# Latent norms of the MLA layer: the last chunk's squares go to the ones-products directly, one strip step later

## The chip, the cores and the metric

The kernel runs on one core of one Trainium2 chip. The metric is device time in microseconds (us) of a whole execution, as the median of several runs. One execution is recorded by the hardware profiler; its rows give start times from the start of the span.

## What is computed

The program is a two-layer encoder trunk on a sequence of 1024 tokens of width 1024, in f32. Layer 0 is differential attention and layer 1 is multi-head latent attention. The change is in layer 1, in the norms of its two latents:

```
proj = h @ w_in
q_a, c_kv, k_pe, z = split(proj, [384, 384 + 256, 384 + 256 + 64])
q  = (_rmsnorm(q_a,  q_a_norm_g)  @ w_q_b)     # 384 features: 3 chunks of 128
kv = (_rmsnorm(c_kv, kv_a_norm_g) @ w_kv_b)    # 256 features: 2 chunks of 128
_rmsnorm(x, g): x * rsqrt(mean(x * x, axis=-1) + 1e-6) * g
```

For each token the squares of all features of a latent are summed. The features lie on partitions here, so the sum over a chunk's 128 features needs a product with ones on TensorE, and the chunks' sums have to be added.

## The kernel before, in words

Every f32 product is made of three fp32r products of 128 x 512 (`mm3`, L186 to L188): high by high, low by high, high by low. `gen_half` makes one output chunk of 128 features by one half of the tokens (512) in eight strip steps, each one `mm3` over 128 input features, so 24 products, and then hands the PSUM bank `acc` to a consumer. The weight strips come by DMA (`wraw`), are cast to their high part by ScalarE (`wh`, L231), and the low part is a subtraction on GpSimd (`wl`, L232).

`lora` makes a latent: strips 1 to 3 for the first (three chunks), 4 and 5 for the second (two chunks), each in two halves. Its consumer `put` copies `acc` to `craw` and squares it, both on ScalarE. For chunk 0 the squares go into the tile `csum`; for every later chunk they go into a tile `csq`, and VectorE adds `csq` to `csum` (L1402). `norm(half)` then makes four small products (128x1, L1407): each takes 128 tokens' columns of `csum` as the stationary operand and a column of ones as the moving one, and puts the sums into the PSUM tile `cps`. VectorE makes `c_w` from it (L1409), GpSimd raises it to the power of minus a half (`rq_y`), two DMAs spread the row over the partitions (`bc_d`, `bc_s`), VectorE scales `craw` (L1416), ScalarE casts its high part (`c_h`, L1424), VectorE subtracts (L1425) and two DMAs write both to `cS`.

There are four norms: two latents by two halves. A norm isn't issued where its chunk ends but within the next half: `half_and_norm` calls what is waiting in `norms` after the strip step with number `NORM_AT` (4, so after five of eight steps). The order of the instructions on each engine is fixed when the program is built; each engine works its list in order and waits at an instruction whose inputs are not there.

Beside the latents VectorE works on `combos`: sums and differences `t1` to `t4` of the input for the gate branch that follows, each with a cast on ScalarE and a subtraction on VectorE (L1341 to L1350). Behind the latents come the first strips of the gate branch (`silu_gate`: `zth` on ScalarE, `gz` on VectorE, L783), then `z_pair`, whose products (`zacc`) take weights that VectorE combines first (`zs`, `zraw`, L1493 to L1496). `load_wk` splits the weights of the values in between (`wvh` on VectorE, `wvl` on GpSimd, L1554 and L1555).

Of the kernel before, what the change touches and what calls it, by code (L numbers as in the profile page):

```python
# [21 lines left out]
P = 128  # L22
# [22 lines left out]
V_LATE = 6  # L45
MODS = (2, 1, 1, 1, 0, 0, 0, 0)
V1_AT = (3, 2)
NORM_AT = 4
PRE0 = (0, 0, 0, 0, 2, 1, 2, 2, 2, 2, 1)
PRE_N = 6  # L50
PRE1 = (0, 0, 0, 0, 0, 0, 0, 1, 1, 1, 1)
# [28 lines left out]
def f32v(ap):  # L80
    return ap.bitcast(F32)
# [3 lines left out]
def trunk(ctx: ExitStack, tc: tile.TileContext, A, out):  # L85
    nc = tc.nc
    SP, PE, V, S, G = nc.sync, nc.tensor, nc.vector, nc.scalar, nc.gpsimd
# [31 lines left out]
    def bank(tag, name, shape=None):  # L119
        nonlocal turn  # L120
        if tag == "acc":
            turn += 1
            if (turn - 1) % (2 + NB.get("accx", 0)) < 2:
                return psa.tile([P, HF], F32, name=name, tag="acc", bufs=2)
            tag = "accx"
        return ps.tile(shape or [P, HF], F32, name=name, tag=tag, bufs=NB[tag])
# [19 lines left out]
    ones = const.tile([P, P], F32, name="ones")  # L146
# [23 lines left out]
    def rsqrt(w, n):  # L170

        y = sm.tile([P, n], F32, name="rq_y")
        G.tensor_tensor(out=y, in0=w, in1=mhalf[:, :n], op=ALU.pow)
        return y
# [231 lines left out]
    def bcast_rows(sp, y, tag, bufs):  # L406

        d_ = dr.tile([HF], F32, name="bc_d", tag="bcd", bufs=4)
        SP.dma_start(d_.rearrange("(p t) -> p t", p=P), y)
        b = sp.tile([P, HF], F32, name="bc_s", tag=tag, bufs=bufs)  # L410
        SP.dma_start(b, d_[None, :].to_broadcast([P, HF]))
        return b, b.rearrange("p (q t) -> p t q", t=4)

    def t3(ap_):
        return ap_.rearrange("p (t q) -> p t q", t=4)
# [838 lines left out]
    w4, h1f, lm = [], {}, {}  # L1254

    def strip1(i, wpool=None):
        return load_strip([A["w_s1"][i, f] for f in range(2)], [4, 4], wpool)
# [40 lines left out]
    def rpt(name, dt=F32):  # L1298
        return wp.tile([P, HF], dt, name=name, tag="rp", bufs=6)
# [76 lines left out]
    def run_norms():  # L1376
        for f in norms[:]:
            norms.remove(f)
            f()

    def half_and_norm(w, half, consume):

        for k, _ in enumerate(gen_half(w, h1, half, consume)):
            side.tick()
            if k == NORM_AT:
                run_norms()

    def lora(idx, dst, gvec, width, ws=None, first=None):
        n = len(idx)
        craw = [[None, None] for _ in range(n)]  # L1390
        sums = [None, None]
        def put(i, half, acc):
            t = rpt("craw") if dst and i == 0 else lr.tile([P, HF], F32, name="craw", tag="craw", bufs=7)
            S.copy(t, acc)
            craw[i][half] = t
            if i == 0:
                sums[half] = lr.tile([P, HF], F32, name="csum", tag="csum", bufs=2)
                lm["S"] = S.activation(sums[half], acc, AF.Square).ins
            else:
                s2 = rpt("csq")  # L1400
                lm["S"] = S.activation(s2, acc, AF.Square).ins
                lm["V"] = V.tensor_add(sums[half], sums[half], s2).ins  # L1402

        def norm(half):
            pt = bank("tr", "cps", [P, 4, P])
            for j in range(4):
                PE.matmul(pt[:, 0, j : j + 1], sums[half][:, j * P : (j + 1) * P], ones[:, 0:1], start=True, stop=True)  # L1407
            wv = sm.tile([P, 4], F32, name="c_w")
            V.tensor_scalar(wv, pt[:, 0, 0:4], 1.0 / width, EPS, op0=ALU.mult, op1=ALU.add)  # L1409
            y = rsqrt(wv, 4)  # L1410
            _, rb = bcast_rows(wp, y, "rp", 6)

            def rest():
                for i in range(n):
                    t = craw[i][half]
                    tc.keep_in_program_order(V.scalar_tensor_tensor(  # L1416
                        out=t3(t), in0=t3(t), scalar=gvec[:, i : i + 1], in1=rb, op0=ALU.mult, op1=ALU.mult))
                norms.append(split)

            def split():  # L1420
                for i in range(n):
                    t = craw[i][half]
                    hi = p4.tile([P, HF], F32R, name="c_h", tag="zraw", bufs=6)
                    S.copy(hi, t)  # L1424
                    V.tensor_sub(t.bitcast(F32R), t, f32v(hi))  # L1425
                    SP.dma_start(cS[dst + i, half, 0], f32v(hi))
                    SP.dma_start(cS[dst + i, half, 1], t)

            norms.append(lambda: norms.append(rest))

        for i, si in enumerate(idx):
            w = strip1(si) if i or ws is None else ws
            for half in range(2):
                if (i, half) == (0, 0) and first:
                    first(lambda acc: put(0, 0, acc))
                else:
                    half_and_norm(w, half, lambda acc: put(i, half, acc))
                if i == n - 1:
                    norms.append(lambda half=half: norm(half))
# [18 lines left out]

    p4 = None
    lora((1, 2, 3), 0, qag, QL, w4[1], first_halves)  # L1460
    zraw = []

    def z_fetch(p, parts):
        for m, f in parts:
            raw = p4.tile([P, HF], F32, name="zraw", tag="zraw", bufs=6)
            SP.dma_start(raw, A["w_s1"][6 + 2 * p + m, f])
            zraw.append(raw)

    lora((4, 5), 3, kvg, KVL)
    for h in range(2):  # L1470
        w = strip1(6 + h)
# [417 lines left out]
    class Pre7:  # L1889
        n = 0  # L1890
# [295 lines left out]
```

## Time and profile before

| what | value |
|---|---|
| median of three runs | 1426.74 us (1424.81 to 1427.36) |
| the profiled execution's own time | 1425.08 us |
| its span | 1423.3 us |
| granted TensorE clock over the span | 0.996 |
| PE busy, VectorE busy, ScalarE busy, GpSimd busy | 1387.4, 935.2, 730.0, 658.4 us |
| first and last start of the four norms' small products | 828.1 and 865.3 us |

In the rows PE is TensorE's matmul, PEld its weight load, DVE is VectorE, ACT ScalarE, POOL GpSimd, SP the engine that issues the DMAs. A row of the timeline has start, duration, engine, source line, operation, output and inputs, shape, and in square brackets how long the engine sat idle before it and who ended that. Spacing between two starts on PE is the better measure of what a product costs, since the shown ends are modelled and overlap the next product.

### The profile page before, as it was taken

Reading aid. Unit: us, or ns where it says so; the run is one execution under the profiler, and the core shown is the slowest. Engines: PE = TensorE matmul, PEld = TensorE weight load, DVE = VectorE, ACT = ScalarE, POOL = GpSimd, SP = SyncE. Lnnn points to the kernel's source line nnn. Section 1 sums busy time; section 2 is a strip of 40 time slices with the busy share of each in tenths; the row PEclk is TensorE's granted clock in tenths of the full one; section 3 lists DMA queues with packets and bytes.
Section 4 is the critical chain, followed back from the end, with each engine's and each line's share of the span. In section 5 each row is a group of like instructions: output and inputs, shape, how many; then the busy total and the mean of one; then the engine's idle time right before and its main releaser. Section 6 shows DMA issues by size and latency. Waiting matters only on the chain. (4 is left out here: it accounts for less than half of the span.)

```text
span 1423.3 us, 20684 instructions
## 1 busy us (share of the span) xinstructions
PE 1387.4 (97%) x7366; PEld 1155.7 (81%) x7366; DVE 935.2 (66%) x1364; ACT 730.0 (51%) x1299; POOL 658.4 (46%) x520
## 2 busy tenths in 40 slices
PE   9999999999999999998999999999999999999997
PEld 6777788888888887886788777887888888888886
DVE  8665777777777777677435886545666655555685
ACT  5523465656565655566343543335454454545554
POOL 5425254646464646453561324532131165653683
PEclk9999999999999999999999999999999999999999
DMA  9786633333332323236572136398544355566363
GB/s 346 246 244 199 192 88 112 82 112 104 111 112 89 90 90 90 89 101 232 201 221 108 55 111 203 121 301 239 158 124 120 101 166 185 182 212 210 130 252 119
DMA packets 141722, 222.35 MB, mean 156 GB/s; under 512 B 19762, under 2 KB 56754, under 8 KB 141619
## 3 DMA queue, kind: packets, MB, share of 16 engines
q1 hardware_dynamic: 141618, 221.03, 49.2%
q8 instruction: 58, 0.95, 0.3%
q14 instruction: 46, 0.37, 0.1%
HBM read 141.07 MB, written 56.31 MB: 139 GB/s over the span
## 5 line engine op out<-in xcount | busy, mean ns | idle before, releaser
L386 ACT CAST pth<-tr 128x512 fp32r<-128x512 f32 x256 | 150.1, 586 | 288.0 <-PE tr L384 286.2
L401 DVE TENSOR_REDUCE nm<-s 128x1 f32<-128x1024 f32 x192 | 234.0, 1219 | 73.3 <-PE s L848 61.5
L387 DVE TENSOR_TENSOR ptl<-tr,pth 128x512 fp32r<-128x512 f32 x256 | 176.1, 688 | 140.4 <-ACT pth L386 139.8
L232 POOL TENSOR_TENSOR wl<-wraw,wh 128x512 fp32r<-128x512 f32 (+2 forms) x79 | 104.9, 1330 | 211.3 <-ACT wh L231 198.8
L403 ACT ACTIVATE e<-s,nm 128x1024 f32<-128x1024 f32 x128 | 143.6, 1122 | 28.8 <-DVE nm L401 26.6
L384 PE MATMUL tr<-ident,e 128*128 128x128 f32 x1024 | 155.7, 274 | 2.4 <-DVE ptl L387 2.1
L384 PEld LDWEIGHTS tr<-ident,e 128*128 128x128 f32 x1024 | 121.3, 140 | 44.3 <-DVE ptl L387 20.2
L186 PE MATMUL acc<-h0h,wh 128*128 128x512 f32 x360 | 149.8, 416 | 1.1 <-ACT wh L231 0.6
L186 PE MATMUL pv<-pth,vt 128*128 128x256 f32 x512 | 147.8, 289 | 0.0
L187 PE MATMUL pv<-ptl,vt 128*128 128x256 f32 x512 | 145.8, 285 | 0.0
L188 PE MATMUL pv<-pth,vt 128*128 128x256 f32 x512 | 144.6, 282 | 0.0
L188 PE MATMUL acc<-h0h,wl 128*128 128x512 f32 x360 | 143.2, 398 | 0.4 <-POOL wl L232 0.4
L187 PE MATMUL acc<-h0l,wh 128*128 128x512 f32 x360 | 141.9, 394 | 0.0
L187 PEld LDWEIGHTS pv<-ptl,vt 128*128 128x128 f32 x512 | 97.6, 191 | 3.0 <-DVE ptl L387 0.2
L186 PEld LDWEIGHTS pv<-pth,vt 128*128 128x128 f32 x512 | 97.5, 190 | 3.0 <-ACT pth L386 0.4
L188 PEld LDWEIGHTS pv<-pth,vt 128*128 128x128 f32 x512 | 97.5, 191 | 0.1
L328 POOL TENSOR_TENSOR rp_r<-rp_raw,cosT 128x512 f32<-128x512 f32 x38 | 50.0, 1315 | 89.7 <-ACT rp_raw L325 37.9
L333 POOL TENSOR_TENSOR rp_sw<-rp_sw,sinT 128x512 f32<-128x512 f32 x42 | 55.4, 1319 | 70.5 <-DMA rp_sw<-rp_raw 68.0
L848 PE MATMUL s<-ks,qa 128*128 128x512 f32 x256 | 82.3, 403 | 3.8 <-DVE e L856 2.2
L856 DVE SCALAR_TENSOR_TENSOR e<-s,z,e 128x1024 f32<-128x1024 f32 x64 | 82.1, 1283 | 2.0
L848 PE MATMUL s<-ks,qb 128*128 128x512 f32 x256 | 80.7, 396 | 0.0
L188 PEld LDWEIGHTS acc<-h0h,wl 128*128 128x128 f32 x360 | 67.6, 188 | 16.1 <-POOL wl L232 0.8
(505 smaller groups left out, 3406.7 us busy)
## 6 DMA issues: line engine op xcount, KB each, us to landing
ada<-in_ada_ss SPq DMA_DIRECT2D x32, 512.0 KB, 5.6
wraw<-in_w_s SPq DMA_DIRECT2D x64, 256.0 KB, 2.9
vS<-v_hl SPq DMA_DIRECT2D x32, 512.0 KB, 5.9
vt<-vS SPq DMA_DIRECT2D x32, 512.0 KB, 4.3
rp_sw<-rp_raw SPq DMA_DIRECT2D x168, 64.0 KB, 2.0
bc_s<-bc_d SPq DMA_DIRECT2D x34, 256.0 KB, 3.8
wor<-in_w_out SPq DMA_DIRECT2D x32, 256.0 KB, 4.3
wol<-tS SPq DMA_DIRECT2D x28, 256.0 KB, 4.9
```

The source lines that it names most:

```text
L186: PE.matmul(psum, ah, bh, start=first, stop=False, skip_group_check=skip)
L187: PE.matmul(psum, ah, bl, start=False, stop=False, skip_group_check=skip)
L188: mm3.last = PE.matmul(psum, al, bh, start=False, stop=last, skip_group_check=skip).ins
L232: sub = (V if pair_of else G).tensor_sub(l_[:, :n], raw[:, :n], f32v(h_[:, :n]))
L333: in_turn(G.tensor_mul(sw, sw, sinT[:, cs]))
L384: PE.transpose(tr[:, j, :], p[:, kt * P : (kt + 1) * P], ident)
L386: mk["S"] = S.copy(pth[kh][:, :, dst], tr).ins
L387: mk["V"] = V.tensor_sub(ptl[kh][:, :, dst], tr, f32v(pth[kh][:, :, dst])).ins
L401: mk["V"] = V.reduce_max(nm, s_ps, axis=AX.X, negate=True).ins
L403: mk["S"] = S.activation(e, s_ps, AF.Exp, bias=nm, scale=1.0, accum_out=zs).ins
L848: PE.matmul(s_ps[:, kc * HF : (kc + 1) * HF], src[:, c, ql], KS[h][kc][:, c, :], start=fst, stop=not fst)
L856: combined.append(V.scalar_tensor_tensor(out=e0, in0=e1, scalar=z1[:, 0:1], in1=e0, op0=ALU.mult, op1=ALU.add).ins)
```

## The change

In a latent's last chunk the squares are no longer added to `csum` on VectorE. They stay in their own tile, and `norm` makes eight small products in place of four: for each 128 tokens one with `csum` and one with the last chunk's `csq`, summed in PSUM. For the first latent that leaves one addition per half on VectorE, for the second latent none. `NORM_AT` goes from 4 to 5, so that a norm is issued after six of eight strip steps.

```
-NORM_AT = 4
+NORM_AT = 5
...
-        sums = [None, None]
+        sums, last = [None, None], [None, None]
...
                 lm["S"] = S.activation(s2, acc, AF.Square).ins
-                lm["V"] = V.tensor_add(sums[half], sums[half], s2).ins
+                if i < n - 1:
+                    lm["V"] = V.tensor_add(sums[half], sums[half], s2).ins
+                else:
+                    last[half] = s2
...
             for j in range(4):
-                PE.matmul(pt[:, 0, j : j + 1], sums[half][:, j * P : (j + 1) * P], ones[:, 0:1], start=True, stop=True)
+                for t in (sums[half], last[half]):
+                    PE.matmul(pt[:, 0, j : j + 1], t[:, j * P : (j + 1) * P], ones[:, 0:1], start=t is sums[half], stop=t is last[half])
```

On TensorE, at the first norm (first latent, first half), the four small products stood three large products earlier; now eight stand there, by turns from `csum` and `csq` (the first two pairs' rows are shown, lines with + are of the changed kernel):

```order
 L188 MATMUL acc<-h1h,wl 128x512
-L1407 MATMUL cps<-ones,csum 128x1 x4
 L186 MATMUL acc<-h1h,wh 128x512
 L187 MATMUL acc<-h1l,wh 128x512
 L188 MATMUL acc<-h1h,wl 128x512
+L1412 MATMUL cps<-ones,csum 128x1
+L1412 MATMUL cps<-ones,csq 128x1
+L1412 MATMUL cps<-ones,csum 128x1
+L1412 MATMUL cps<-ones,csq 128x1
```

The norm moved one strip step back, and its second product is the first that needs the last chunk's squares. The second and third norms move in the same way. The fourth stood behind the last strip step of its half; now its first product stands after six steps and the other seven after one more step and one product.

On VectorE, in the stretch ahead of the third norm (second latent, first half), the addition to `csum` stood behind the scaling of three chunks of the first latent:

```order
-L1425 TENSOR_TENSOR craw<-craw,c_h 128x512 x3
-L1416 SCALAR_TENSOR_TENSOR craw<-craw,vec,bc_s 128x512 x3
-L1402 TENSOR_TENSOR csum<-csum,csq 128x512
-L1346 TENSOR_TENSOR t4f<-h_7h,t2f 128x512
+L1430 TENSOR_TENSOR craw<-craw,c_h 128x512
+L1421 SCALAR_TENSOR_TENSOR craw<-craw,vec,bc_s 128x512 x3
+L1350 TENSOR_TENSOR t4f<-t4f,h_7l 128x512
+L1346 TENSOR_TENSOR t3f<-h1f_8008,h1f_7990 128x512
```

The addition is gone and work on `combos` has moved up in its place. Further on, at the start of the gate branch, VectorE combines the weights for the first `z_pair`. Before (a `zs` with its number is one tile):

```order
L1493 TENSOR_TENSOR zs_8763<-zraw 128x512
L1494 TENSOR_TENSOR zraw<-zraw 128x512
L783 SCALAR_TENSOR_TENSOR gz<-zth,acc 128x512
L1495 TENSOR_TENSOR zraw<-zs_8763,zraw 128x512
L1554 CAST wvh<-wvr 128x512
```

and now:

```order
L1498 TENSOR_TENSOR zs_8775<-zraw 128x512
L1499 TENSOR_TENSOR zraw<-zraw 128x512
L1500 TENSOR_TENSOR zraw<-zs_8775,zraw 128x512
L1501 TENSOR_TENSOR zraw<-zraw 128x512
L783 SCALAR_TENSOR_TENSOR gz<-zth,acc 128x512
```

The step that makes the next weight (L1495 before, L1500 now) no longer has the gate's `gz` ahead of it. On GpSimd, at the same place of the program, the low parts of the gate weights (`wl`) and of the value weights (`wvl`) stood so before:

```order
L232 TENSOR_TENSOR wl<-zraw,wh 128x512 x2
L1555 TENSOR_TENSOR wvl<-wvr,wvh 128x512
L232 TENSOR_TENSOR wl<-zraw,wh 128x512
L1555 TENSOR_TENSOR wvl<-wvr,wvh 128x512
L232 TENSOR_TENSOR wl<-zraw,wh 128x512
```

and now:

```order
L232 TENSOR_TENSOR wl<-wraw,wh 128x512
L232 TENSOR_TENSOR wl<-zraw,wh 128x512 x3
L1560 TENSOR_TENSOR wvl<-wvr,wvh 128x512 x2
L232 TENSOR_TENSOR wl<-zraw,wh 128x512
L232 TENSOR_TENSOR wl<-zs_8775,wh 128x512
```

The third `wl` of the gate weights has moved ahead of both `wvl`. Outside of this stretch, from the first `csq` to the first `z_pair`, each engine has the same instructions in the same order, up to line numbers and tile numbers.

## Prediction

> **What bounds the kernel.** I read the page first, then the list of who waited for whom on TensorE, then PE's timeline at the norms.
>
> ```profile
> PE 1387.4 (97%) x7366; PEld 1155.7 (81%) x7366; DVE 935.2 (66%) x1364; ACT 730.0 (51%) x1299; POOL 658.4 (46%) x520
> ```
>
> ```profile
> PE cps L1407 <- DVE csum L1402: 3.1, 2, 2.1
> ...
> PE zacc L188 <- POOL wl L232: 1.4, 1, 1.4
> ...
> PE vps L186 <- DVE v_hl L364: 1.3, 1, 1.3
> ```
>
> PE is busy 97% of the span, so the time is PE's work plus PE's waits. The first row of the waits is the one the change aims at: PE stood at the small products twice, 3.1 us together, for VectorE's addition. The other two rows lie further on and decide whether time won here stays won. Here are the first norm, with a wait, the second, without, and the third, with one:
>
> ```profile
> 826.69 0.39 PE L188 MATMUL acc<-h1h,wl 128*128 128x512 f32 x1
> 828.11 1.02 PE L1407 MATMUL cps<-ones,csum 128*128 128x1 f32 x8 [1.02 <-DVE csum L1402]
> 828.99 0.48 PE L186 MATMUL acc<-h1h,wh 128*128 128x512 f32 x1
> ...
> 831.38 0.39 PE L187 MATMUL acc<-h_0l,wh 128*128 128x512 f32 x1
> ...
> 834.40 0.40 PE L188 MATMUL acc<-h_4h,wl 128*128 128x512 f32 x1
> 834.63 0.95 PE L1407 MATMUL cps<-ones,csum 128*128 128x1 f32 x8
> 835.44 0.48 PE L186 MATMUL acc<-h_5h,wh 128*128 128x512 f32 x1
> ...
> 851.90 0.39 PE L188 MATMUL acc<-h1h,wl 128*128 128x512 f32 x1
> 854.38 1.02 PE L1407 MATMUL cps<-ones,csum 128*128 128x1 f32 x8 [2.09 <-DVE csum L1402]
> 855.26 0.48 PE L186 MATMUL acc<-h1h,wh 128*128 128x512 f32 x1
> ...
> 859.22 0.39 PE L187 MATMUL acc<-h_0l,wh 128*128 128x512 f32 x1
> ```
>
> The reader is to see the spacing. From the last large product ahead of a norm to the first behind it, it is 1.04 us where nothing waits (834.40 to 835.44). It is 2.30 at the first norm and 3.36 at the third. Behind the third, ten large products take 3.96 us (855.26 to 859.22), where behind the first the same ten take 2.39 (828.99 to 831.38). The reason is in the table of windows:
>
> ```profile
> 671.42:674.83 3.41, 1.14 (x4) 0.48 (x3) 2.41 (x4) 2.48 (x5) 3.41 (x3) 1.00 0.23 81
> 674.83:678.24 3.41, 3.13 (x10) 2.46 (x10) 1.02 (x1) 0.00 (x0) 2.69 (x3) 0.50 0.67 216
> ...
> 852.33:855.74 3.41, 1.36 (x10) 1.35 (x11) 3.41 (x6) 1.76 (x3) 0.82 (x1) 1.00 0.72 280
> 855.74:859.15 3.41, 3.41 (x10) 2.64 (x9) 3.41 (x6) 1.07 (x2) 3.41 (x2) 0.50 0.53 197
> ...
> 886.44:889.86 3.42, 2.04 (x9) 1.38 (x8) 2.73 (x4) 2.42 (x5) 3.41 (x3) 1.00 0.43 153
> ```
>
> Columns are the stretch, its length, PE's busy time, then PEld, DVE, ACT and POOL, then the granted clock. After a window of 3.41 us with only 1.14 or 1.36 us of PE work the clock is 0.50 for the next such window. After one with 2.04 it stays at 1.00. So the long wait of the third norm was paid twice, as idle time and as slow products behind it.
>
> **The change, part by part.**
>
> *Taken away: the waits.* Why they go is in the squares on ScalarE and the additions on VectorE:
>
> ```profile
> 826.63 0.60 ACT L1401 ACTIVATE csq<-acc 128x512 f32<-128x512 f32 x1
> ...
> 832.16 0.60 ACT L1401 ACTIVATE csq<-acc 128x512 f32<-128x512 f32 x1
> ...
> 849.39 0.60 ACT L1401 ACTIVATE csq<-acc 128x512 f32<-128x512 f32 x1
> ...
> 859.70 0.60 ACT L1401 ACTIVATE csq<-acc 128x512 f32<-128x512 f32 x1
> ```
>
> ```profile
> 827.27 0.69 DVE L1402 TENSOR_TENSOR csum<-csum,csq 128x512 f32<-128x512 f32 x1 [0.29 <-ACT csq L1401]
> ...
> 850.40 3.23 DVE L1416 SCALAR_TENSOR_TENSOR craw<-craw,vec,bc_s 128x512 f32<-128x512 f32 x3
> 853.54 0.69 DVE L1402 TENSOR_TENSOR csum<-csum,csq 128x512 f32<-128x512 f32 x1
> ```
>
> At the first norm the square ends at 827.23 and nothing ahead of it on ScalarE or VectorE has moved. PE comes to the small products one strip step later than now, at 826.69 + 4 x 0.23 = 827.61, so nothing is left to wait for; the margin is 0.4 us. At the third norm the square ends at 849.99, but the addition sat behind 3.23 us of scaling until 854.2. Without it PE would find its square 1.9 us old at 851.90, and it now comes a step later still. The second and fourth squares are 1.9 and 4.3 us old where PE takes them. So both waits go: (2.30 - 1.04) + (3.36 - 1.04) = **3.58 us**.
>
> *Taken away: the slow clock* behind the third norm, 3.96 - 2.39 = **1.57 us**.
>
> *Added: sixteen small products*, four per norm. Four cost 0.81 us (834.63 to 835.44). No row has eight in succession; below, they can't be free, since PE takes them in order between large products, and above I take the 0.88 of a group that had waited (828.11 to 828.99). I take 0.81, since that group ran unhindered: 4 x 0.81 = 3.24. The fourth norm is split in two, which is one more return to large products at 835.76 - 835.44 = 0.32 in place of 0.23 by the row below: **3.33 us**, between 3.2 and 3.6.
>
> ```profile
> 835.76 0.40 PE L187 MATMUL acc<-h_5l,wh 128*128 128x512 f32 x1
> ```
>
> *Moved: the rest of the norm.* The sums reach VectorE later by a strip step and the added products, 1.5 us; from there on run `c_w`, the power on GpSimd, two DMAs, scaling, casts and writes. The first half's scaling should still not come later: ahead of it on VectorE stands a subtraction that waits for a cast, and ScalarE's list now has that cast earlier. The normed latent is read back from DRAM only in the last `z_pair`, tens of us on, which covers all of this. Four additions on VectorE (0.69 each) go as well; they count only through the waits above, since VectorE isn't the bound. On ScalarE's list casts `c_h` now stand ahead of a copy that empties a PSUM bank; five banks cover that.
>
> Up to the gate branch PE is thus ahead by 3.58 + 1.57 - 3.33 = **1.82 us**.
>
> *Moved: the start of the gate branch.* There PE next waits:
>
> ```profile
> 883.42 0.69 DVE L1493 TENSOR_TENSOR zs<-zraw 128x512 f32<-128x512 f32 x1 [4.10 <-DMA cS<-c_h]
> 884.14 0.69 DVE L1494 TENSOR_TENSOR zraw<-zraw 128x512 f32<-128x512 f32 x1
> 884.75 0.68 DVE L783 SCALAR_TENSOR_TENSOR gz<-zth,acc 128x512 f32<-128x512 f32 x1
> 885.35 0.68 DVE L1495 TENSOR_TENSOR zraw<-zs,zraw 128x512 f32<-128x512 f32 x1
> ```
>
> ```profile
> 886.07 0.62 ACT L231 CAST wh<-zraw 128x512 fp32r<-128x512 f32 x1 [3.28 <-DVE zraw L1495]
> ```
>
> ```profile
> 886.45 1.68 POOL L1555 TENSOR_TENSOR wvl<-wvr,wvh 128x512 fp32r<-128x512 f32 x1 [4.43 <-DVE wvh L1554]
> 888.10 1.45 POOL L232 TENSOR_TENSOR wl<-zraw,wh 128x512 fp32r<-128x512 f32 x1
> ```
>
> ```profile
> 887.82 0.40 PE L187 MATMUL zacc<-t2l,wh 128*128 128x512 f32 x1
> 889.60 0.50 PE L188 MATMUL zacc<-t2h,wl 128*128 128x512 f32 x1 [1.38 <-POOL wl L232]
> ```
>
> The chain is DMA, `zs`, `zraw`, `gz`, `zraw`, `wh`, then `wvl` in the way, then `wl`, then PE. It cost 889.60 - 887.82 - 0.23 = 1.55 us. In the new order `gz` (0.60) is out of it and `wvl` as well: `wl` could begin at 886.8, right after the cast, in place of 888.10, so 1.3 us. That is 1.9 us of chain gone against 1.55 of wait. If the chain's head moves up with PE, the wait ends. The head was a write of `c_h`, whose cast is held by PE's own progress:
>
> ```profile
> 876.80 0.60 ACT L782 ACTIVATE zth<-acc 128x512 f32<-128x512 f32 x1 [3.91 <-PE acc L188]
> 877.29 1.13 ACT L1424 CAST c_h<-craw 128x512 fp32r<-128x512 f32 x2
> ```
>
> Those casts stand directly behind a `zth` that waits for PE, so they come 1.8 us earlier too. I take the whole **1.55 us**; its bounds are 0, if the write lands where it did, and 1.55. What is late next is the following `wl`, which stands behind both `wvl` as before and moves up with them.
>
> *Behind that* all orders are unchanged, and loads and casts are released by PE's progress, so I carry the lead to the end.
>
> **Sum.** 1.82 + 1.55 = 3.37 us off the profiled execution's 1425.08 gives 1421.71. That execution lies 1.66 under the median of the runs shown, so for the median it is 1426.74 - 3.37 = **1423.4**.
>
> **A rule of the skill.** The rows have the clock halved for one window of 3.41 us after a window with a third of its time in work. The Trainium skill, page "TensorE: Matmul & The Clock Gate", Part 1 on the HAM clock gate, has the clock fall to half after at least one idle window of about 3.4 us, with windows that run freely. The trace agrees on the half and on the length, and not on idle: both windows that were followed by 0.50 held over 1 us of PE work. By the rule as it stands the change could cause no drop at all, and the sum stays 1423.4; by the trace, see the second rival.
>
> **The rivals.**
>
> *The gate branch keeps its wait* (20%). `zs` waits for a DMA, and the same writes may land when they did. Then only 1.82 us remain: **1424.9**.
>
> *Small products count as rest for the clock* (6%). A norm now holds 1.62 us of small products in one go; a window around it has 3.41 - 1.62 = 1.79 us of large ones. The bar lies between 1.14, which was followed by a drop, and 2.04, which wasn't. For: 1.79 is inside. Against: it is near the upper end, and a group can straddle two windows. A drop costs 1.57; all four give -3.37 + 6.28: **1429.7**; two give 1426.5.
>
> *The wait moves to ScalarE* (9%), the case on the slower side. The products need the square itself, which stands in ScalarE's list behind casts `c_h` that wait for the scaling, which waits for `bc_s`. If that chain is late by more than the 1.9 us that the third square has in hand, plus the step of 0.7, PE waits as before, with the clock's drop behind it, and pays the sixteen products on top: 1426.74 + 3.33 = **1430.1**. Against: before, the same casts stood ahead of that square and it was still ready at 849.99.
>
> *The lead grows* (10%). The third wait quoted first, 1.3 us for `v_hl`, hangs on DMAs for the rotation; if they come early by more than PE, it goes too: **1422.1**.
>
> *The lead is lost* (5%) to the same wait, if those DMAs don't move with PE: about **1426.7**.
>
> **How the numbers follow.** The forecast, 1423.4, has 50%, with 1422.4 to 1424.6 as its own range. A measurement of this kernel can tell about 0.2%, 2.85 us, from no change, so faster means under 1423.9. Two thirds of the forecast (33%), all of the grown lead and 1% of the first rival are faster: 44%. The moved wait and half of the clock rival are slower: 12%. The rest is 44%. The range reaches from the grown lead less the 0.8 that the runs scatter, 1421.3, to the lost lead plus as much, 1427.5; outside lie the moved wait and three or more drops of the clock.
>
> **What would show it.** In the changed profile PE should have no wait at L1412; from the large product ahead of a norm to the one behind it should be 1.8 to 1.9 us; the granted clock should be 1.00 through 820 to 900; large products ahead of the first `zacc` should start about 1.8 us earlier than 881.99, and the wait at the third `zacc` should be gone. I am wrong if PE waits for ScalarE's `csq`, if a window of 0.50 follows a norm, or if a wait near 974 grows by what was won.
>
> ```profile
> 881.99 0.40 PE L186 MATMUL zacc<-h_0h,wh 128*128 128x512 f32 x1
> ```

## The result, and the profile after

The changed kernel has a median of 1424.08 us (12 runs, 1421.77 to 1425.91), the kernel before, beside it, 1426.84 us. The ratio is 0.9977 with a 95% interval of 0.9967 to 0.9986, so 3.3 us less, 2.0 to 4.7. The forecast was 1423.4, with 1421.3 to 1427.5 as its range. The profiled execution is the slowest of the twelve: own time 1425.91, span 1424.1. It can't be set beside the 1425.08 of before as a whole, because it reached the changed stretch late, in code that is the same in both. So I measure the stretch by itself, from the first product of the latents' stage to the first product of the values, which lies behind all that moved. Here is PE's timeline of the kernel before at these two places:

```profile
778.97 0.39 PE L186 MATMUL acc<-h_0h,wh 128*128 128x512 f32 x1
...
941.79 0.39 PE L186 MATMUL vps<-wvh,ckh 128*128 128x512 f32 x1
```

and of the changed kernel, with the first gate product between them (881.99 before, in the prediction):

```profile
781.83 0.39 PE L186 MATMUL acc<-h_0h,wh 128*128 128x512 f32 x1
...
883.20 0.40 PE L186 MATMUL zacc<-h_0h,wh 128*128 128x512 f32 x1
...
942.72 0.39 PE L186 MATMUL vps<-wvh,ckh 128*128 128x512 f32 x1
```

Up to the first gate product it was 881.99 - 778.97 = 103.02 us, now it is 101.37: **1.65 less** (forecast 1.82). From there to the first value product it was 59.80, now 59.52: **0.28 less** (forecast 1.55). Together the stretch went from 162.82 to 160.89 us, **1.93 less** (forecast 3.37).

On the page PE's busy time grew by 1.8 us, with 32 more records (two for each of the sixteen products):

```profile
PE 1389.2 (98%) x7398; PEld 1158.6 (81%) x7398; DVE 935.2 (66%) x1360; ACT 730.0 (51%) x1299; POOL 656.3 (46%) x520
```

In the list of PE's waits there is none at the small products any more. The one at the gate branch has the same 1.4 us as before, and the one for `v_hl` its 1.3:

```profile
PE zacc L188 <- POOL wl L232: 1.4, 1, 1.4
...
PE vps L186 <- DVE v_hl L364: 1.3, 1, 1.3
```

PE's timeline at the first norm, at the third, and at the fourth, which is split:

```profile
830.23 0.39 PE L188 MATMUL acc<-h1h,wl 128*128 128x512 f32 x1
830.46 0.28 PE L1412 MATMUL cps<-ones,csum 128*128 128x1 f32 x2
830.60 0.36 PE L1412 MATMUL cps<-ones,csq 128*128 128x1 f32 x2
...
832.16 0.49 PE L186 MATMUL acc<-h1h,wh 128*128 128x512 f32 x1
...
855.95 0.39 PE L188 MATMUL acc<-h1h,wl 128*128 128x512 f32 x1
...
857.88 0.49 PE L186 MATMUL acc<-h1h,wh 128*128 128x512 f32 x1
...
863.31 0.39 PE L188 MATMUL acc<-h_5h,wl 128*128 128x512 f32 x1
...
863.67 0.48 PE L186 MATMUL acc<-h_6h,wh 128*128 128x512 f32 x1
...
864.45 0.39 PE L186 MATMUL acc<-h_7h,wh 128*128 128x512 f32 x1
...
866.16 0.48 PE L187 MATMUL acc<-h_7l,wh 128*128 128x512 f32 x1
```

From large product to large product it is 832.16 - 830.23 = 1.93 us at the first norm, 1.93 at the third, and at the fourth 0.36 and 1.71. No row has a bracket, so PE waits for nothing. The windows around the first and the third norm show the clock:

```profile
829.78:833.20 3.42, 3.42 (x25) 3.11 (x24) 3.35 (x5) 1.47 (x3) 1.53 (x1) 1.00 0.01 2
...
853.68:857.09 3.41, 3.41 (x21) 2.98 (x20) 3.41 (x5) 0.42 (x2) 0.00 (x0) 1.00 0.44 150
857.09:860.51 3.42, 3.42 (x20) 2.94 (x20) 3.42 (x7) 3.42 (x8) 0.87 (x1) 1.00 0.51 195
```

It is 1.00 in all three; the window of 0.50 behind the third norm is gone. What did not go is the wait at the gate branch. VectorE, ScalarE, GpSimd and PE there, one after another:

```profile
884.51 0.69 DVE L1498 TENSOR_TENSOR zs<-zraw 128x512 f32<-128x512 f32 x1 [3.98 <-DMA cS<-c_h]
```

```profile
886.74 1.14 ACT L231 CAST wh<-zraw 128x512 fp32r<-128x512 f32 x2 [2.75 <-DVE zraw L1500]
```

```profile
887.44 1.30 POOL L232 TENSOR_TENSOR wl<-zraw,wh 128x512 fp32r<-128x512 f32 x1 [2.90 <-ACT wh L231]
889.10 2.66 POOL L1560 TENSOR_TENSOR wvl<-wvr,wvh 128x512 fp32r<-128x512 f32 x2 [0.36 <-DVE wvh L1559]
891.72 1.72 POOL L232 TENSOR_TENSOR wl<-zraw,wh 128x512 fp32r<-128x512 f32 x1
```

```profile
891.75 0.39 PE L187 MATMUL zacc<-t3l,wh 128*128 128x512 f32 x1
893.49 0.50 PE L188 MATMUL zacc<-t3h,wl 128*128 128x512 f32 x1 [1.35 <-POOL wl L232]
```

The head of the chain moved up as forecast: 884.51 is 102.68 behind the stage's first product, 883.42 was 104.45. The low part of the third gate product's weights is ready at 888.74, and nothing waits there. But both `wvl` now stand ahead of the fourth product's `wl`, and PE waits for that one: 893.49 - 891.75 - 0.23 = 1.51 us, where it was 1.55 at the third. **The wait moved on by one product.**

### The profile page after: what moved, and what is told of

It reads as the page before. It is cut to its first block, busy times and chain, and to the rows that moved or that the text cites. A ratio compares the mean times of both kernels' runs of the same rounds, so it can differ in the third digit from the quotient of the medians.

```text
span 1424.1 us, 20739 instructions
## 1 busy us (share of the span) xinstructions
PE 1389.2 (98%) x7398; PEld 1158.6 (81%) x7398; DVE 935.2 (66%) x1360; ACT 730.0 (51%) x1299; POOL 656.3 (46%) x520
## 4 chain that ended last, share of the span: by engine, by line
PE 82%; DVE 6%; DMA 4%; ACT 3%; POOL 2%; issue 2%; SPq 0%; ACTq 0%; POOLq 0%; DVEq 0%
PE s L1753 10%; PE acc L188 8%; PE acc L186 8%; PE acc L187 8%; PE tr L384 8%; PE s L848 7%; PE pv L187 4%; PE pv L188 4%; PE pv L186 4%; PE oacc L187 2%; PE oacc L188 2%; PE oacc L186 2%; PE vps L186 1%; PE zacc L188 1%; PE vps L188 1%
```

## The experiments

All lengths are read as above, in us, from the first product of the latents' stage (start) to the first gate product, from there to the first value product, and the sum. Times and ratios are against the kernel before on the same chip.

| run | start | to the gate | gate to values | sum | ratio to before (95%) |
|---|---|---|---|---|---|
| before | 778.97 | 103.02 | 59.80 | 162.82 | |
| changed | 781.83 | 101.37 | 59.52 | 160.89 | 0.9977 (0.9967 to 0.9986) |
| later step alone | 782.70 | 101.89 | 60.74 | 162.63 | 0.9999 (0.9987 to 1.0011) |
| products alone | 782.37 | 102.79 | 58.39 | 161.18 | 0.9983 (0.9968 to 0.9999) |
| changed, `wvl` on VectorE | 787.12 | 101.36 | 58.18 | 159.54 | 0.9972 (0.9957 to 0.9986) |
| changed, four products | 784.26 | 98.30 | 60.57 | 158.87 | 0.9968 (0.9956 to 0.9981) |
| changed, rows tripled | 781.55 | 131.66 | 57.88 | 189.54 | 1.0172 (1.0156 to 1.0189) |
| addition on GpSimd | 783.82 | 110.35 | 58.13 | 168.48 | 1.0050 (1.0036 to 1.0064) |
| changed, again | 784.64 | 101.35 | 59.51 | 160.86 | 0.9977 (0.9967 to 0.9988) |
| before, second profile | 780.41 | 104.59 | 59.15 | 163.74 | |
| third norm only, `wvl` on VectorE | 782.52 | 99.81 | 60.52 | 160.33 | 0.9995 (0.9979 to 1.0010) |
| changed, `wvl` on VectorE, again | 779.80 | 101.36 | 57.92 | 159.28 | 0.9969 (0.9958 to 0.9980) |
| before, third profile | 778.92 | 104.76 | 59.54 | 164.30 | |
| before, fourth profile | 780.82 | 103.18 | 59.32 | 162.50 | |

The column "start" is worth a look. All code ahead of it is the same in all fourteen, and it ranges over 8.2 us (4.8 among the six profiles of one chip). That scatter lies in every whole time, and it is why the stretch is the better witness.

**The later step alone** (kernel before, the additions kept).

```
-NORM_AT = 4
+NORM_AT = 5
```

> The kernel before with the norm one strip step later and nothing else: the additions stay on VectorE, four small products per norm. If each part does what the prediction says: the first norm's sum is ready at about 827.9 on the clock of the profile before, and PE comes one step later at 827.6, so of its wait of 1.26 us at most 0.4 is left; at the third norm the addition still stands behind three scalings and ends at about 854.2, so PE waits 2.3 us there again, and a window of clock 0.50 may follow. At the gate branch the third low part now stands ahead of the value weights, so the wait of 1.55 goes or moves on to the fourth product with 0 to 1.3. In time 1.0 to 2.5 us under the kernel before. Rival, that the later step alone ends both waits: no wait at the small products, no slow window, 5.1 us or more under the kernel before.

PE's timeline at the first and third norm, and the window around the third:

```profile
831.83 1.02 PE L1407 MATMUL cps<-ones,csum 128*128 128x1 f32 x8 [0.34 <-DVE csum L1402]
...
857.44 1.32 PE L1407 MATMUL cps<-ones,csum 128*128 128x1 f32 x8 [1.43 <-DVE csum L1402]
```

```profile
854.63:858.04 3.41, 1.98 (x13) 1.43 (x11) 3.41 (x5) 1.01 (x2) 2.84 (x1) 1.00 0.40 151
858.04:861.45 3.41, 3.41 (x11) 2.83 (x11) 3.41 (x6) 1.66 (x3) 3.41 (x2) 0.50 0.00 0
```

The first wait shrinks to 0.34, the third stays with 1.43 and still has a window of 0.50 behind it. The third is shorter than the 2.3 I expected: PE stands there at the same time behind the stage's start as before, and the addition is done 0.67 us earlier (857.44 - 782.70 against 854.38 - 778.97). The step alone does not end the waits. Of what it wins up to the gate, 1.13, the gate branch takes 0.94 back (60.74 for 59.80), with waits of 0.63 and 0.86 for `wl` and 0.22 for `wh`: the head of its chain, `zs`, starts at 888.66, 105.96 behind the stage's start, where it was 104.45. Its time is that of before within 0.13%, not the 1.0 to 2.5 us less that I expected.

**The products alone** (the changed kernel at the old step).

```
-NORM_AT = 5
+NORM_AT = 4
```

> The changed kernel with the norm at its old step (after five of eight): the products with the last chunk's squares stay. If the products take the waits away by themselves: the first norm waits 0.2 to 0.4 us for the square on ScalarE (ready at 827.23, PE there at about 826.9), the third not at all, clock 1.00 behind both, eight small products 1.6 to 1.9 us. From the first product of the latents' stage to the first gate product within 0.4 us of the changed kernel's 101.37 (before: 103.02). In time 1.5 to 2.5 us under the kernel before. Rival, that the later step is what matters: a wait of 1 us or more at the first or third norm, and no gain.

ScalarE ahead of the third norm, and PE at it:

```profile
854.79 0.62 ACT L1429 CAST c_h<-craw 128x512 fp32r<-128x512 f32 x1 [3.66 <-DVE craw L1421]
855.85 0.62 ACT L1429 CAST c_h<-craw 128x512 fp32r<-128x512 f32 x1 [0.44 <-DVE craw L1421]
...
856.85 0.60 ACT L1402 ACTIVATE csq<-acc 128x512 f32<-128x512 f32 x1
```

```profile
856.27 0.28 PE L1412 MATMUL cps<-ones,csum 128*128 128x1 f32 x2
857.51 0.38 PE L1412 MATMUL cps<-ones,csq 128*128 128x1 f32 x2 [0.97 <-ACT csq L1402]
```

I expected no wait at the third norm, and that was wrong. Here the rival that put the wait on ScalarE is what happens: the square stands behind two casts of the second half, which wait for VectorE's scaling (3.66 us), and PE waits 0.97 for the square. In the changed kernel ScalarE's list has the square ahead of the second half's casts:

```profile
852.76 0.60 ACT L1402 ACTIVATE csq<-acc 128x512 f32<-128x512 f32 x1
...
857.38 1.66 ACT L1429 CAST c_h<-craw 128x512 fp32r<-128x512 f32 x3
```

It ends at 853.36, 2.8 us before PE is through with the last large product ahead of that norm (855.95 + 0.23). So it takes both parts to end both waits: the products to get rid of VectorE, and the later step for what it does to ScalarE's order. In time the later step adds little. Without it the stretch is 161.18 us, 0.29 over the changed kernel: PE is 1.42 later at the gate and waits 0.21 there at the fourth product in place of 1.35. By whole times the two can't be told apart.

**`wvl` on VectorE** (the changed kernel; nothing but these two subtractions moves).

```
-            G.tensor_sub(l_, raw, f32v(h_))
+            (V if fh else G).tensor_sub(l_, raw, f32v(h_))
```

> The changed kernel with the two subtractions wvl of the value weights on VectorE in place of GpSimd; nothing else moves. If the wait of 1.5 us at the fourth gate product is there because both wvl (2.66 us on GpSimd) stand ahead of its wl: that wl ends at about 890.0 in place of 893.44, PE (there at 891.98) does not wait, the first value product comes 1.5 us earlier, and the end too: 1.3 to 1.6 us under the changed kernel, 3.4 to 5 under the kernel before. The later wait of 1.3 us for v_hl stays as it is, since it hangs on PE's own product. Rival, that the wait hangs on the DMA at the chain's head or on the cast: it stays within 0.3 of 1.5. Second rival, that the lead is lost behind: the wait goes, and another of 1.0 us or more shows before the end of the attention's first head.

GpSimd and PE at the gate branch:

```profile
893.24 2.75 POOL L232 TENSOR_TENSOR wl<-zraw,wh 128x512 fp32r<-128x512 f32 x2 [2.92 <-ACT wh L231]
```

```profile
897.33 0.39 PE L187 MATMUL zacc<-t3l,wh 128*128 128x512 f32 x1
897.56 0.39 PE L188 MATMUL zacc<-t3h,wl 128*128 128x512 f32 x1
```

The two `wl` now follow each other, and PE goes through the fourth product at its pace of 0.23. The gate part is 1.34 shorter, as expected. From the first value product to the layer's first product with `pv` it is 53.14 us, 53.18 in the changed kernel, so what is won here is carried on. Repeated beside the third-norm run:

> The changed kernel with wvl on VectorE once more, beside the run with the products in the third norm only. If its first profile is the rule: 101.3 to 101.5 us from the first product of the stage to the first gate product, 159.4 to 159.7 to the first value product, no wait for wl; 2.8 to 4.2 us under the kernel before. If the wait's end was chance: a wait of over 0.5 us at one of the first four gate products.

The wait is gone again, and the sum is 159.28, just under what I expected. By the stretch this is the best of the versions that compute the same, 1.35 to 1.6 us under the changed kernel. By whole times its ratio and the changed kernel's overlap, so device times can't tell the two apart.

**Four small products** (the changed kernel without the last chunk's squares).

```
-                for t in (sums[half], last[half]):
-                    PE.matmul(pt[:, 0, j : j + 1], t[:, j * P : (j + 1) * P], ones[:, 0:1], start=t is sums[half], stop=t is last[half])
+                PE.matmul(pt[:, 0, j : j + 1], sums[half][:, j * P : (j + 1) * P], ones[:, 0:1], start=True, stop=True)
```

> The changed kernel without the products with the last chunk's squares (it leaves these squares out of the norms' sums): four small products per norm at the later step. This prices the sixteen added products: the forecast has 3.33 us (3.2 to 3.6). From the large product ahead of a norm to the one behind it 1.04 in place of 1.8 to 1.9; from the first product of the latents' stage to the first gate product 98.0 us (changed kernel 101.37); 3.3 us under the changed kernel if nothing is late next, about 6 under the kernel before. Rival, that small products in a longer row overlap or that they pay for a drain elsewhere: a difference of 1.6 us or less. Rival, that the gate branch's wait takes it back: the stretch to the first gate product is 3.3 shorter, but the wait at the third and fourth gate product grows by 1 us or more.

```profile
832.66 0.39 PE L188 MATMUL acc<-h1h,wl 128*128 128x512 f32 x1
...
833.70 0.49 PE L186 MATMUL acc<-h1h,wh 128*128 128x512 f32 x1
...
862.13 0.40 PE L187 MATMUL acc<-h_4l,wh 128*128 128x512 f32 x1
862.69 0.50 PE L188 MATMUL acc<-h_4h,wl 128*128 128x512 f32 x1 [0.16 <-POOL wl L232]
```

The spacing is 1.04 again. Up to the gate it is 3.07 shorter, and 0.33 more was lost to a wait for `wl` that the changed kernel has not (862.69 - 862.13 - 0.23), so sixteen products cost 3.4 us. The gate part is 1.05 longer: PE comes earlier, and the weights are not there earlier. A third of that is more wait at the fourth product (1.69 in place of 1.35), the rest are stalls of 0.3 and 0.35 at the first and the third. So the rival that the gate branch takes a part back holds too, spread over three products.

**Rows tripled** (the changed kernel, each row of eight done three times).

```
-                for t in (sums[half], last[half]):
-                    PE.matmul(pt[:, 0, j : j + 1], ...
+                for r in (2, 1, 0):
+                    for t in (sums[half], last[half]):
+                        PE.matmul(pt[:, r, j : j + 1], ...
```

> The changed kernel with each norm's row of eight small products done three times, twice into columns that nobody reads: 24 in a row, 64 more in all. At the 0.222 us between two starts that the changed kernel's rows show, a norm takes 24 x 0.222 + 0.15 = 5.5 us from large product to large product, so that at least one whole stretch of 3.41 us holds small products alone. If small products count as work for the clock: 1.00 throughout, 64 x 0.222 = 14.2 us longer from the first product of the stage to the first gate product (115.6 for 101.37), and some 12 to 15 us slower than the changed kernel. If they count as rest (the second rival of the prediction): a window of 0.50 behind, or within, each of the four norms, 1.5 us or more each on top, 18 us or more slower than the changed kernel.

Four windows from the first norm on:

```profile
829.34:832.75 3.41, 3.41 (x29) 3.25 (x27) 3.34 (x5) 1.50 (x3) 1.52 (x1) 1.00 0.00 0
832.75:836.16 3.41, 3.41 (x18) 3.41 (x17) 2.65 (x5) 0.00 (x0) 0.00 (x0) 0.50 0.26 77
836.16:839.57 3.41, 3.41 (x14) 3.12 (x14) 1.40 (x3) 0.00 (x0) 1.20 (x1) 0.50 0.00 0
839.57:842.98 3.41, 3.41 (x10) 2.64 (x9) 0.37 (x2) 2.46 (x5) 1.47 (x2) 0.50 0.02 1
```

PE is busy for the whole of the first window and never idle, and still the clock is 0.50 in the next three. The row begins at 830.19, so the first window holds 0.85 us of large products and 2.56 of small ones. Behind each of the four norms two or three windows are at 0.50, and the stretch to the gate is 30.3 us longer where the products by themselves are 14.2. So small products are rest to the clock: the second rival's mechanism is real, and eight in a row (1.70 us) are not enough for it.

**The addition on GpSimd** (the kernel before, with `wvl` on VectorE and the norm after seven steps).

```
-NORM_AT = 4
+NORM_AT = 6
...
-                lm["V"] = V.tensor_add(sums[half], sums[half], s2).ins
+                if i < n - 1:
+                    lm["V"] = V.tensor_add(sums[half], sums[half], s2).ins
+                else:
+                    G.tensor_add(sums[half], sums[half], s2)
...
```

> The kernel before with three edits: the last chunk's square is added to the sum on GpSimd in place of VectorE, the norm is issued after seven of eight strip steps, and wvl is made on VectorE as in the run with it. Four small products per norm, none added. If the prediction's terms are right: waits at the first and third norm 0 to 0.5 us (the addition takes 1.3 on GpSimd behind a square that is ready two steps earlier), no slow window, the sixteen products saved: from the first product of the stage to the first gate product 98.0 to 99.0 us (before 103.02, changed 101.37), gate wait 0 to 0.3, in all 5.5 to 6.5 us under the kernel before. Rival, that the addition on GpSimd delays the weights' low parts behind it: a wait for wl of 1 us or more in the latents, and no more gain than the run with wvl on VectorE.

GpSimd's additions for the second and the third norm, and PE's wait at the third:

```profile
842.37 1.26 POOL L1405 TENSOR_TENSOR csum<-csum,csq 128x512 f32<-128x512 f32 x1
...
859.43 6.83 POOL L1405 TENSOR_TENSOR csum<-csum,csq 128x512 f32<-128x512 f32 x1 [4.94 <-ACT csq L1401]
```

```profile
866.31 1.87 PE L1410 MATMUL cps<-ones,csum 128*128 128x1 f32 x8 [3.31 <-POOL csum L1405]
```

This fails, and neither of my two accounts had the reason. At the third norm the addition takes 6.83 us in place of 1.3, and PE waits 3.31 with two slow windows behind it. At the second it is short, but stands behind the power `rq_y` (839.51) and a `wl` (840.94), and PE waits 2.89; at the first PE waits 0.75. The rival's wait for `wl` in the latents does not show. The kernel is 0.5% slower than before.

**The products in the third norm only** (with `wvl` on VectorE).

```
-                if i < n - 1:
+                if i < n - 1 or n == 3 or half:
...
```

> The changed kernel with wvl on VectorE, and with the products from the last chunk's square only in the third norm; at the first, second and fourth the addition on VectorE is back and four small products stand there. By the prices measured so far: the first norm waits 0.3 us for the addition as in the run with the later step alone, twelve small products are saved (12 x 0.22 = 2.6 us), gate wait 0. On ScalarE three casts c_h stand ahead of the third square again, as in the run with the products alone, so PE waits there too if that order is what made it wait: 0.3 to 1.2 us at the third norm with a step of 0.69 more in hand. From the first product of the stage to the first gate product 99.3 to 100.5 us (changed 101.37), to the first value product 157.5 to 158.7; 4.5 to 5.5 us under the kernel before. Rival, that the square's lateness in the run with the products alone came from the step and not from the casts: no wait at the third norm, 99.0 or less.

Up to the gate it does what the prices say (99.81). The third norm does not wait: the casts ahead of its square are those of the first half, which were done, and not those of the second half as in the run with the products alone; I had taken them for the same. But the gate part gives 2.3 us back against the run with `wvl` on VectorE. PE waits for `wl` at the first and the third gate product (0.63 and 0.87), and ahead of the third for `wh` (0.22). The chain's head, `zs`, starts at 886.40, 103.88 behind the stage's start, where it is 102.68 in the changed kernel: VectorE has two subtractions of `craw` and a `gz` ahead of it. So the sum is 160.33 and not the 157.5 to 158.7 that I expected, the interval of its ratio holds 1, and it is no better than the changed kernel with `wvl` on VectorE.

**Both kernels again**, with no edit.

> The changed kernel once more, on this chip, beside the others. If what its profile showed is the rule: no wait at the small products, no slow window from 820 to 900, 101.2 to 101.6 us from the first product of the stage to the first gate product and 160.6 to 161.2 to the first value product, one wait of 1.2 to 1.5 us at the fourth gate product; 1.5 to 3.5 us under the kernel before. If the gain of its median beyond 1.9 us came from earlier parts of the program: 1.9 us or less here.

> The kernel before once more, for a second profile. If the slow window behind the third norm is the rule: waits of 1.0 and 2.1 us at the first and third norm again and a window of clock 0.50 that begins within 3.41 us of the second, 103.0 us from the first product of the stage to the first gate product, 162.8 to the first value product. Rival, that windows fall freely and the long wait is often split between two: the same waits, no slow window, 101.5 us to the first gate product.

> The kernel before, a third profile. What is open is why the medians differ by more than the 1.93 us that the first profiles show. If the number of slow windows behind the third norm varies with where the free windows fall: waits of 1.0 and 2.1 us again, one or two windows of 0.50 behind the third norm, or none where the wait is split over two windows, and from the first product of the stage to the first value product 161.2 (none), 162.8 (one) or 163.7 us (two). Rival, that the second profile's 163.7 was a stray: 162.8 within 0.2.

> The kernel before, a fourth profile, with the same expectation as the third: 161.2, 162.8 or 163.7 us from the first product of the stage to the first value product with none, one or two slow windows behind the third norm; by the rival 162.8 within 0.2 each time.

The changed kernel repeats itself within 0.03 us over the stretch. The kernel before doesn't. Here are the windows behind the third norm of its second profile:

```profile
852.72:856.13 3.41, 1.31 (x8) 0.84 (x6) 3.41 (x5) 2.21 (x4) 0.00 (x0) 1.00 0.85 325
856.13:859.55 3.42, 3.42 (x12) 2.95 (x12) 3.42 (x8) 0.79 (x2) 3.17 (x1) 0.50 0.42 158
859.55:862.96 3.41, 3.41 (x9) 2.64 (x8) 2.23 (x3) 1.83 (x4) 3.41 (x3) 0.50 0.46 163
```

The wait is the same 2.1 us, but two windows follow at 0.50. The third profile has two as well, so the second was no stray; the fourth has one. With one, the stretch to the gate is 103.02 and 103.18 us; with two, 104.59 and 104.76. Whether the gate branch hides a part of that isn't clear: its wait is 1.38 and 0.91 us behind one window, 0.73 and 1.13 behind two.

## Why the prediction was right and where it was wrong

*The waits go: right.* Neither profile of the changed kernel has a wait at L1412, and the spacing is 1.93 where 1.8 to 1.9 was forecast.

*The slow clock goes: right, but mis-sized.* The price of 1.57 is that of one window. In two of four profiles of before there were two, which makes about 3.1. The forecast read one execution as the rule.

*Sixteen products, 3.33 us: right.* By the rows they are 3 x (1.93 - 1.04) + (0.36 + 1.71 - 2 x 0.23 - 0.81) = 3.47, and leaving them out gave 3.4. The product that opens a row is short (0.14), each later one takes 0.22.

*1.82 us ahead at the gate: 1.65.* The missing 0.17 is nearly all the 0.14 on the products.

*The gate branch's wait, 1.55: wrong; 0.28 came.* The head of the chain moved up by 1.77, as said, and the third product's wait ended. The step that failed is the sentence on what comes next: that the following `wl` "stands behind both `wvl` as before and moves up with them". It did move up, 1.9 us: its end was 892.49 by the sum of the rows 890.75 and 1.74 of before, 113.52 behind the stage's start, and is 893.44 now, 111.61 behind it. But PE, freed at the third product, came to it 3.34 us earlier: 892.23 + 0.23 of before is 113.49 behind the start, 891.75 + 0.23 now is 110.15. Before, the wait at the third product had paid for the fourth. These are GpSimd's rows of before that follow the two in the prediction:

```profile
889.50 1.29 POOL L1555 TENSOR_TENSOR wvl<-wvr,wvh 128x512 fp32r<-128x512 f32 x1
890.75 1.74 POOL L232 TENSOR_TENSOR wl<-zraw,wh 128x512 fp32r<-128x512 f32 x1
```

The GpSimd work up to the fourth `wl` was the same in both orders, two `wl` and two `wvl` (from 886.45 to 892.49 before, from 887.44 to 893.44 now), and only an order was changed. The runs with `wvl` on VectorE show it: with that work off GpSimd the wait ends, and the 1.34 to 1.6 us are there.

*Carried to the end: right.* From the first value product to the first `pv` it is 53.15 us before and 53.18 after, and the wait for `v_hl` is 1.32 and 1.29. From there to the end of the span it is 428.4 and 428.2. The rivals of a grown and a lost lead both fall.

*The rival "the gate branch keeps its wait" (1424.9)* is what happened, though not by its reason: the DMA was not late, GpSimd's queue was. *The wait on ScalarE* did not come in the changed kernel; the run with the products alone shows how near it was. *Small products as rest* did not come either, for eight in a row.

So the predicted 1423.4 is near the measured 1424.08 in part by luck, by two errors against each other: too much at the gate branch, and too little for the slow clock. Over four profiles of before and two of the changed kernel the part up to the gate is 103.89 and 101.36 us, so 2.53 less where 1.82 was forecast; the gate part is 59.45 and 59.52, so nothing less where 1.55 was forecast.

Over its four profiles the kernel before takes (162.82 + 163.74 + 164.30 + 162.50) / 4 = 163.34 for the stretch, 2.46 over the changed kernel's 160.88. The medians differ by 2.76, and the interval of the ratio, 2.0 to 4.7, holds 2.46. From the start of the stretch to the end of the span the profiles of before have 644.3, 645.7, 646.3 and 644.5 us, those of the changed kernel 642.3 and 642.2, which is 3.0 less on average and near the 3.3 of the ratio. About half of the 0.5 us that lies behind the stretch stands ahead of the first `pv`, where PE waits 0.26 and 0.37 us for a DMA (`vt`) in the second and fourth profile of before, and in no other of these. Whether the change has a part in that isn't shown, and how often one window or two follow the third norm is known from four profiles only.

*The clock's bar.* The prediction put it between 1.14 and 2.04 us of PE work in a window. The runs narrow it if only large products are counted. Followed by 0.50: the window of 1.98 us of PE work with the later step alone, whose large products end at 855.62 + 0.23, so 1.22 us after its start at 854.63; and 0.85 with the rows tripled. Not followed by a drop: the changed kernel's 829.78 to 833.20, 3.42 us less a row of 1.70, so 1.72. Two more windows narrow it further. With the addition on GpSimd the one from 842.43 to 845.85 has large products from 844.60 on, 1.25 us, and the next is 0.50; with the products alone the one from 830.22 to 833.63 has a row of small ones from 830.31 to 832.25, so 1.47 us of large ones, and the next is 1.00. The bar lies between 1.25 and 1.47. In the Trainium skill, page "TensorE: Matmul & The Clock Gate", Part 1 on the HAM clock gate, the clock falls after an idle window of about 3.4 us, and the windows run freely. The trace agrees on the freely running windows; on "idle" it does not, since the window from 829.34 to 832.75 was busy for 3.41 of 3.41 us.

## What to carry to other kernels

When a reordering frees a wait on a shared queue, add up the queue's whole work to the next consumer as well: if that sum is unchanged, the wait can move on by one consumer and not end. Here only work taken off the queue got it back. Price a wait that drags the clock down with it as a range, and ask what share of a window is large products, since rows of 128x1 products counted as rest here. And where unchanged code ahead scatters more than the effect, measure between two marks in the trace.

## What the runs showed of the hardware

*A product of 128x1 keeps PE busy and lets its clock fall.* Behind a window with 2.56 us of them the clock was 0.50, and they then came every 0.43 us in place of 0.22 (starts at 832.84 and 833.26 in the run with the rows tripled). At 0.50 a window counts for less: in the second profile of before, the window from 856.13 has PE busy throughout, with 2.2 us of large products at half speed (from 857.29 on), and the next is 0.50 again. With the later step alone the window from 858.04 has 2.8 us of them (from 858.62 on), and the next is 1.00. At half speed these are the work of 1.1 and 1.4 us, an estimate that fits the bar above.

*GpSimd's addition took 1.26 us in one place and 6.83 in another.* In the long one VectorE worked without a gap on instructions with two inputs from SBUF, first its scalings, then sums for `combos` and the low parts up to 865.1:

```profile
857.05 3.27 DVE L1419 SCALAR_TENSOR_TENSOR craw<-craw,vec,bc_s 128x512 f32<-128x512 f32 x3
860.23 0.69 DVE L1346 TENSOR_TENSOR t4f<-h_7h,t2f 128x512 f32<-128x512 f32 x1
```

The Trainium skill, page "GPSIMD Engine Reference", section 1 on the specifications, has GpSimd's SBUF interfaces shared with VectorE, with contention for instructions of VectorE with two SBUF inputs. The 6.83 us agree with that: the addition ended at 866.26, 1.1 us after VectorE's row (865.14), about what it takes by itself, as if it had run only then. In the same run it happened the other way round too: beside a `wl` on GpSimd (850.50, 1.29 us) the scaling that VectorE began at 850.54 took 2.18 us, where those ahead of it followed each other in 1.06. No run here took VectorE's work away from beside the addition, so it isn't shown to be the cause.
